# Deeper load buffers for the second part of a hybrid SSD and GLA layer, paid for with DMA scratch

## The chip, the cores and the metric

The kernel runs on one core of a Trainium2 chip. The metric is the device time of one execution in microseconds (us). Lower is better. Engines are named as in the profile: PE is TensorE (matmuls; PEld its weight loads), DVE is VectorE, ACT is ScalarE, POOL is GpSimd, SP is SyncE, which here only issues DMAs.

## The reference: what is computed

One layer of a hybrid decoder with 2048 tokens (and 16 meta tokens ahead of them) and a width of 1024. A normalised input is projected into all branch inputs; two branches (an SSD scan and a gated linear attention scan) give `y_ssd` and `y_gla`; then the branches are projected, gated, added and projected again:

```python
u = rmsnorm(hres, norm_w)
proj = jnp.einsum('bld,dn->bln', u, w_in)          # merge_g is the last 2048 of its columns
...                                                # the two scans give y_ssd and y_gla
branches = jnp.stack([y_ssd, y_gla], axis=2)
branch_proj = jnp.einsum('blnc,ncd->blnd', branches, w_branch)
gates = jax.nn.sigmoid(merge_g.reshape(b, l, N_BRANCH, D_MODEL))
merged = jnp.sum(gates * branch_proj, axis=2)
h = hres + jnp.einsum('bld,de->ble', merged, w_out)
return rmsnorm(h, final_norm_w)[:, N_META:]
```

## The kernel before, in words

The kernel has two parts. The first computes the branch inputs and the scans and leaves `u` and the two `y` in DRAM. The second part, which alone is changed, does the gate projection, the two branch projections and the output projection as large matrix products.

**The second part.** It has seven stages in this order: for each half of the tokens a gate stage, the first branch stage and the second branch stage, then one output stage. Each stage multiplies a right operand of 1024 x 1024 (all its quarters and their sums and differences stay in SBUF for the whole stage) with a left operand that passes by in pairs of row blocks. It does so by a seven product scheme (a 2 x 2 Strassen scheme in Winograd's form): the order of products for each two pairs is `PS = (1, 2, 6, 7, 5, 3, 4)`, each for the one pair and then the other, so that a stage of eight pairs has 56 products and one of four pairs has 28; 280 products in all. A product is 12 matmuls of 128x128 by 128x512: four contraction tiles by three, since every operand is held as a high and a low float32r half.

**What feeds a product.** A right operand tile is loaded raw by SP (`load_b`, line 966, tile `br`), and split by ACT (high half, line 971) and DVE (low half, line 972) into a tile `b`; 28 of them make a stage. The left operand comes by `load_a` (line 978, tile `ar`), POOL makes sums and differences of its quarters (lines 986 to 989, tiles `as`), and ACT and DVE split each into a tile `a` (lines 995 and 996) five products ahead. Products 1, 6, 5 and 3 of a pair gather in the same PSUM bank (`psa`): after product 1, 6 and 5 ACT copies what stands there to SBUF (line 1012, tile `sn`, called the snapshot below), and the next product of that pair may only go on in the bank when the copy is done. Between product 5 of a pair and its product 3 lies one product of the other pair. What comes out is used by the stage's epilogue, for which SP loads gates, partial sums or rows of the input into tiles `io` (lines 1043, 1045 and 1068).

**Who sets the order.** PE's and SP's instructions run in the order of the code. A list of positions sets it: `load_b` for the 28 tiles of the next stage stands at positions from 12 products ahead of the stage on, 0.8 products apart (`pos`), less a lead; `prep_b`, the split, stands at `pos`. The order on ACT, DVE and POOL is made when the program is built, by a scheduler that estimates times. SP's queue is in order: a load that waits for its buffer holds all the loads behind it. Each tile name has a ring of buffers (`bufs`), so a load waits until the tile that many loads back has been read for the last time. Besides, all DMAs of SP and ACT share eight semaphores in turn, and a DMA waits until the one that used its semaphore before has landed.

**Scratch.** A part of SBUF of 16 KB per partition is set aside for descriptors of DMAs that POOL issues. There are two of these in the whole program: the last two stores of `y` (line 878).

Of the kernel before, what the change touches and what calls it, by code (L numbers as in the profile page):

```python
# [7 lines left out]
F32 = mybir.dt.float32  # L8
# [6 lines left out]
P = 128  # L15
# [3 lines left out]
BLK = 512  # L19
# [21 lines left out]
def trunk_kernel(ctx: ExitStack, tc: tile.TileContext, xm, xmt, w_feat, w_tok, w_zm, w_br, w_o,  # L41
                 cf32, cmsk, pvec, fnw, hvec, gw2, out):
    nc = tc.nc
# [5 lines left out]
    def mk(pool, shape, dt, tag, **kw):  # L49
        cnt[0] += 1  # L50
        return pool.tile(shape, dt, tag=tag, name=f"{tag}_{cnt[0]}", **kw)
# [20 lines left out]
    def make_sums(pool, tag, nb, braw, sums, j, c, store):  # L72
        cs = slice(c * HB, (c + 1) * HB)
        pair = [mk(pool, [P, 512], F32, tag, bufs=nb).rearrange("p (i c) -> p i c", i=2) for _ in range(2)]
        for r, (k, t) in zip((t[:, i] for t in pair for i in range(2)), ((0, 1), (0, 0), (1, 1), (1, 0))):
            nc.sync.dma_start(r, braw(4 * k + j, t)[:, cs])
        yield
        (b12, b11), (b22, b21) = [(t[:, 0], t[:, 1]) for t in pair]
        for o, x, y in ((b11, b12, b11), (b12, b22, b12), (b22, b22, b11), (b21, b21, b22)):
            nc.gpsimd.tensor_tensor(o, x, y, op=ALU.subtract)  # L80
        if store is None:
            for dst, src in zip(sums, pair):
                late_store(dst[j][:, :, cs], src, 2)
            return
        yield
        yield
        for dst, src in zip(sums, pair):
            store.dma_start(dst[j][:, :, cs], src)
# [3 lines left out]
    def late_store(dst, src, lag=1):  # L92
        stores.setdefault(step_no[0] + lag, []).append((dst, src))

    def new_sums(name):
        return [[wdram.tile([P, 2, BLK], F32, tag=f"{name}_t{i}_{j}", name=f"{name}_t{i}_{j}", bufs=1)
                 for j in range(4)] for i in range(2)]

    def braw_u(s):
        return lambda k, t: u_left[2 * s + t][k]  # L100

    def braw_y(n, s):
        return lambda k, t: y_left[n][2 * s + t][k]

    def braw_o(k, t):
        return w_o[t, :, k * BLK:(k + 1) * BLK]

    sums = {**{("g", s): (braw_u(s), new_sums(f"gate{s}")) for s in range(nsb)},
            **{("b", n, s): (braw_y(n, s), new_sums(f"br{n}{s}")) for n in range(2) for s in range(nsb)},
            ("o",): (braw_o, new_sums("out"))}  # L110

    beside = {(1, 0): ("o",), (1, 4): ("g", 0)}
    late = []
# [812 lines left out]
    def pool2(name, bufs, **kw):  # L926
        return second.enter_context(tc.tile_pool(name=name, bufs=bufs, reuse_waits="tile", **kw))

    rpl = pool2("raws", 1)
    apl = pool2("aops", 7)  # L930
    bpl = pool2("bops", 4)
    opl = pool2("outs", 1)
# [18 lines left out]
    class Stage:  # L951
# [9 lines left out]
        def load_b(self, p, j):  # L961
            src = {1: lambda j: self.braw(j, 0), 2: lambda j: self.braw(4 + j, 0), 3: lambda j: self.braw(4 + j, 1),
                   4: lambda j: self.sums[1][j][:, 1], 5: lambda j: self.sums[0][j][:, 1],
                   6: lambda j: self.sums[1][j][:, 0], 7: lambda j: self.sums[0][j][:, 0]}[p]
            raw = self.braws[p, j] = mk(rpl, [P, BLK], F32, "br", bufs=5)
            nc.sync.dma_start(raw, src(j))

        def prep_b(self, p, j):
# [5 lines left out]

        def load_a(self, n):
            def raw(i, j):
                t = mk(rpl, [P, 4, P], F32, "ar", bufs=8)
                nc.sync.dma_start(t, self.araw(n, i, j))
                return t

            if n not in self.a:
                self.a[n] = raw(0, 0), raw(0, 1), raw(1, 0)
                return
            (a11, a12, a21), a22 = self.a[n], raw(1, 1)
            s1, s2, s4 = [mk(rpl, [P, 4, P], F32, "as", bufs=6) for _ in range(3)]
            nc.gpsimd.tensor_tensor(s1, a21, a22, op=ALU.add)  # L986
            nc.gpsimd.tensor_tensor(s2, s1, a11, op=ALU.subtract)
            nc.gpsimd.tensor_tensor(a21, a11, a21, op=ALU.subtract)
            nc.gpsimd.tensor_tensor(s4, a12, s2, op=ALU.subtract)
            self.a[n] = {1: a11, 2: a12, 3: s4, 4: a22, 5: s1, 6: s2, 7: a21}  # L990
# [24 lines left out]
                self.use(n, *USES[p], self.ps[n, "b"] if p == 5 else ps, self.snap.get((n, {2: 1, 5: 5, 4: 6}.get(p))))  # L1015

    def io():
        return mk(opl, [P, BLK], F32, "io", bufs=8)

    def total(ps, snap):  # L1020
        if snap is None:
            return ps
        nc.vector.tensor_tensor(snap, snap, ps, op=ALU.add)
        return snap

    def gate_stage(s):
        def use(n, i, t, ps, snap):
            x = total(ps, snap)
            th = io() if snap is None else snap
            nc.scalar.activation(th, x, AF.Tanh, scale=0.5)  # L1030
            store(g_left[2 * s + t][2 * n + i], th)

        return Stage(f"gate{s}", ("g", s), 8,
                     lambda n, i, j: w_feat[T_GATE + 2 * n + i, :, j * BLK:(j + 1) * BLK].rearrange(
                         "p (k c) -> p k c", c=P), use)
# [26 lines left out]
    def out_stage():  # L1062
        fns, res, ssq, done = [], {}, {}, set()

        def fetch(n, i, t):
            r0 = (2 * n + i) * P
            res[n, i, t] = r = io()
            nc.sync.dma_start(r, xm[META + r0:META + r0 + P, t * BLK:(t + 1) * BLK])

        def use(n, i, t, ps, snap):  # L1070
            r0 = (2 * n + i) * P
            r = res[n, i, t]
            done.add((n, i, t))
            x = total(ps, snap)
            nc.vector.scalar_tensor_tensor(r, x, 0.5, r, op0=ALU.mult, op1=ALU.add)
            if (n, i) not in ssq:
                ssq[n, i] = mk(spl, [P, 2], F32, "ssf")
            jk = mk(spl, [P, BLK], BF16, "junk", bufs=1)
            nc.scalar.activation(jk, r, AF.Square, accum_out=ssq[n, i][:, t:t + 1])
            if (n, i, 1 - t) in done:  # L1080
                while len(fns) < 2:
                    fns.append(mk(rpl, [P, BLK], F32, "br", bufs=5))
                    nc.sync.dma_start(fns[-1], fnw[:, (len(fns) - 1) * BLK:len(fns) * BLK].to_broadcast([P, BLK]))
                q = ssq[n, i]
                nc.vector.tensor_tensor(q[:, 0:1], q[:, 0:1], q[:, 1:2], op=ALU.add)
                nc.vector.tensor_scalar(q[:, 0:1], q[:, 0:1], 1.0 / D, EPS, op0=ALU.mult, op1=ALU.add)
                nc.gpsimd.tensor_tensor(q[:, 0:1], q[:, 0:1], mhalf[:, 0:1], op=ALU.pow)
                for hf in range(2):
                    o = res[n, i, hf]
                    nc.vector.scalar_tensor_tensor(o, o, q[:, 0:1], fns[hf], op0=ALU.mult, op1=ALU.mult)  # L1090
                    store(out[r0:r0 + P, hf * BLK:(hf + 1) * BLK], o)

        return Stage("out", ("o",), seq // (2 * P),
                     lambda n, i, j: m_left[(2 * n + i) // 4][j][:, :, (2 * n + i) % 4 * P:((2 * n + i) % 4 + 1) * P],
                     use, fetch, 3)

    stages = []
# [16 lines left out]
    def at(pos, fn):  # L1114
        pos = max(pos, -1)
        todo.setdefault(int(pos // 1), []).append((pos, len(todo), fn))
# [5 lines left out]
    for si, st in enumerate(stages):  # L1122
        for q in range(28):
            p, j = PS[q // 4], q % 4
            pos = begins[si] - 12 + 0.8 * q if si else -0.99 + 0.2 * (q // 4) if q < 16 else 2 * (q // 4 - 4)
            at(pos - (3.2 if si else 0.1), lambda st=st, p=p, j=j: st.load_b(p, j))
            at(pos, lambda st=st, p=p, j=j: st.prep_b(p, j))
    for i, (st, n, p) in enumerate(order):
        if p in USES and st.fetch:
# [2 lines left out]
        at(i - AHEAD if i >= AHEAD else -0.95 + 0.1 * i, lambda st=st, n=n, p=p: st.prep_a(n, p))  # L1132
    begun_at = [begins[3 * s] for s in range(nsb)]
    spots = [g + 9 + 5 * k for g in begun_at for k in range(8)]
    late_sums = [make_sums(opl, "io", 8, *sums[key], j, c, None) for key in late for j in range(4) for c in range(2)]
    for pos, gen in zip(spots, late_sums):
        for k in range(2):
            at(pos + 2 * k, lambda gen=gen: next(gen, None))
# [99 lines left out]
```

## Time and profile before

| | us |
|---|---|
| median of 3 runs | 2309.24 (2306.60 to 2315.05) |
| the profiled execution, its own time | 2308.46 |
| its span in the trace | 2306.7 |
| PE busy | 2232.1 (97% of the span) |
| DVE busy | 1609.6 (70%) |
| ACT busy | 1121.4 (49%) |
| POOL busy | 683.6 (30%) |
| first matmul of the second part | at 1504.6 |
| start of its last matmul | at 2296.4 |

A busy PE says little about how closely its matmuls follow each other: what counts is the time from the start of one matmul to the start of the next, and where it waits. In the tables of windows the columns are the length, then the busy time and the number of instructions of each engine, then the granted clock of PE (1.00 is the full clock), the busy share of the 16 DMA engines and what they moved. In the timelines a number in brackets is the idle time of the engine ahead of the instruction, and what ended it.

### The profile page before, as it was taken

How to read it: one execution, taken by the hardware profiler on the slowest of the kernel's cores; microseconds unless marked ns; L12 is line 12 of the kernel's file. 1: busy time of each engine (PE TensorE's matmuls, PEld its weight loads, DVE VectorE, ACT ScalarE, POOL GpSimd, SP SyncE). 2: the span in 40 equal slices, each digit the busy share in tenths (PEclk: the TensorE clock that was granted, in tenths of full speed). 3: DMA queues.
4: the chain of work that ended last, by engine and by line, in shares of the span. 5: the costliest groups of instructions: out<-in, count | busy, mean ns of one | idle time of the engine just before them, and what ended most of it. 6: DMA issues, size and time to landing. Idle time of an engine off the chain costs nothing.

```text
span 2306.7 us, 36436 instructions
## 1 busy us (share of the span) xinstructions
PE 2232.1 (97%) x12631; PEld 1949.0 (84%) x12631; DVE 1609.6 (70%) x3136; ACT 1121.4 (49%) x2508; POOL 683.6 (30%) x675
## 2 busy tenths in 40 slices
PE   6899999999999999999999999989999999999998
PEld 6899988888888989888988898778787788787886
DVE  5786766687775677676578656664779855778966
ACT  5565554454444445444455334454644545554443
POOL 3344433122221222222122100145424264423341
PEclk9999999999999999999999999999999999999999
DMA  7766865667786676786667644465767866778653
GB/s 260 234 220 219 289 229 205 203 204 230 257 284 193 204 223 213 253 286 215 205 216 230 215 163 156 151 224 200 252 238 261 280 215 217 255 255 273 226 186 110
DMA packets 300809, 515.89 MB, mean 224 GB/s; under 512 B 27616, under 2 KB 143584, under 8 KB 300624
## 3 DMA queue, kind: packets, MB, share of 16 engines
q1 hardware_dynamic: 221840, 422.15, 56.5%
q10 hardware_dynamic: 78624, 90.89, 11.2%
q8 instruction: 99, 1.62, 0.3%
q14 instruction: 86, 0.70, 0.1%
q0 software_dynamic: 160, 0.52, 0.1%
HBM read 366.26 MB, written 147.19 MB: 223 GB/s over the span
## 4 chain that ended last, share of the span: by engine, by line
PE 64%; DVE 12%; DMA 12%; issue 6%; ACT 4%; POOL 1%; SPq 1%; ACTq 0%; DVEq 0%; POOLq 0%
PE pj L189 11%; PE pj L191 11%; PE pj L190 11%; PE psa L189 4%; PE psa L190 4%; PE psa L191 4%; DMA acc<-in_xmt 2%; PE psb L190 2%; PE psb L189 2%; PE psb L191 2%; DMA br<-br_t 2%; PE pc L594 2%; PE pc L758 1%; DVE b L972 1%; PE psc L190 1%
## 5 line engine op out<-in xcount | busy, mean ns | idle before, releaser
L189 PE MATMUL pj<-u,whl 128*128 128x512 f32 (+1 forms) x1184 | 446.0, 377 | 9.5 <-ACT acc L504 4.5
L191 PE MATMUL pj<-u,whl 128*128 128x512 f32 (+1 forms) x1184 | 430.7, 364 | 0.8 <-POOL whl L177 0.8
L190 PE MATMUL pj<-u,whl 128*128 128x512 f32 (+1 forms) x1184 | 430.1, 363 | 0.0
L189 PE MATMUL pj<-whl,u 128*128 128x256 f32 (+1 forms) x992 | 288.7, 291 | 2.4 <-ACT u L252 2.2
L191 PE MATMUL pj<-whl,u 128*128 128x256 f32 (+1 forms) x992 | 282.2, 285 | 0.2 <-DVE u L257 0.2
L190 PE MATMUL pj<-whl,u 128*128 128x256 f32 (+1 forms) x992 | 282.0, 284 | 0.0
L189 PE MATMUL psa<-b,a 128*128 128x512 f32 x640 | 254.0, 397 | 16.4 <-ACT sn L1012 16.2
L189 PEld LDWEIGHTS pj<-u,whl 128*128 128x128 f32 x1184 | 224.5, 190 | 48.4 <-ACT acc L504 5.4
L190 PE MATMUL psa<-b,a 128*128 128x512 f32 x640 | 253.1, 395 | 2.0 <-DVE b L972 2.0
L191 PEld LDWEIGHTS pj<-u,whl 128*128 128x128 f32 x1184 | 224.0, 189 | 36.6 <-POOL whl L177 1.0
L190 PEld LDWEIGHTS pj<-u,whl 128*128 128x128 f32 x1184 | 224.8, 190 | 33.3
L191 PE MATMUL psa<-b,a 128*128 128x512 f32 x640 | 252.6, 395 | 0.0
L996 DVE TENSOR_TENSOR a<-ar,a 128x512 fp32r<-128x512 f32 x160 | 148.1, 930 | 84.3 <-ACT a L995 84.1
L80 POOL TENSOR_TENSOR wr<-wr 128x256 f32<-128x256 f32 x80 | 69.4, 868 | 442.7 <-DMA wr<-u 184.4
L177 POOL TENSOR_TENSOR whl<-wr,whl 128x512 fp32r<-128x512 f32 (+1 forms) x100 | 136.5, 1373 | 195.4 <-ACT whl L176 155.5
L189 PEld LDWEIGHTS pj<-whl,u 128*128 128x128 f32 x992 | 189.6, 191 | 4.1 <-ACT u L252 2.3
L191 PEld LDWEIGHTS pj<-whl,u 128*128 128x128 f32 x992 | 189.6, 191 | 0.8 <-DVE u L257 0.8
L190 PEld LDWEIGHTS pj<-whl,u 128*128 128x128 f32 x992 | 189.8, 191 | 0.4
L972 DVE TENSOR_TENSOR b<-br,b 128x512 fp32r<-128x512 f32 x196 | 148.4, 780 | 43.2 <-ACT b L971 43.1
L986 POOL TENSOR_TENSOR as<-ar,ar 128x512 f32<-128x512 f32 x40 | 59.4, 1484 | 396.2 <-DMA ar<-in_w_br 154.2
L508 DVE SCALAR_TENSOR_TENSOR acc<-cin,hcw,acc 128x512 f32<-128x512 f32 (+1 forms) x192 | 159.6, 831 | 13.9 <-ACT acc L504 11.6
L971 ACT ACTIVATE b<-br 128x512 fp32r<-128x512 f32 x196 | 119.3, 626 | 93.4 <-DMA br<-br_t 41.4
(281 smaller groups left out, 5017.7 us busy)
## 6 DMA issues: line engine op xcount, KB each, us to landing
whl<-k_s SPq DMA_DIRECT2D x96, 512.0 KB, 4.3
whl<-k_g SPq DMA_DIRECT2D x96, 512.0 KB, 4.2
whl<-k_v SPq DMA_DIRECT2D x48, 512.0 KB, 4.0
whl<-k_z SPq DMA_DIRECT2D x36, 512.0 KB, 4.1
wr<-in_w_feat SPq DMA_DIRECT2D x64, 256.0 KB, 4.3
k_s<-whl SPq DMA_DIRECT2D x32, 512.0 KB, 3.7
cb<-cumd ACTq DMA_DIRECT2D x64, 256.0 KB, 5.7
k_g<-whl SPq DMA_DIRECT2D x32, 512.0 KB, 3.9
```

The lines of the kernel that those rows point to most:

```text
L80: nc.gpsimd.tensor_tensor(o, x, y, op=ALU.subtract)
L177: nc.gpsimd.tensor_tensor(hl[:, 1], raw, hl[:, 0].bitcast(F32), op=ALU.subtract)
L189: nc.tensor.matmul(ps, sh, mh, start=first, stop=False, **kw)
L190: nc.tensor.matmul(ps, sh, ml, start=False, stop=False, **kw)
L191: nc.tensor.matmul(ps, sl, mh, start=False, stop=last, **kw)
L508: nc.vector.scalar_tensor_tensor(acc, cin[:, k:k + tt], hcw[:, ti, k:k + 1], acc, op0=ALU.mult, op1=ALU.add)
L594: nc.tensor.matmul(py[:, h * 64:(h + 1) * 64], dm[:, h], xdt[:, h], start=True, stop=True)
L758: nc.tensor.matmul(ps[:, r * P:(r + 1) * P], kq[:, 2 * r * P:(2 * r + 1) * P], kq[:, (2 * r + 1) * P:(2 * r + 2) * P], start=True, stop=True)
L971: nc.scalar.activation(t[:, 0], raw, AF.Copy)
L972: nc.vector.tensor_tensor(t[:, 1], raw, t[:, 0].bitcast(F32), op=ALU.subtract)
L986: nc.gpsimd.tensor_tensor(s1, a21, a22, op=ALU.add)
L996: nc.vector.tensor_tensor(t[:, 1], src, t[:, 0].bitcast(F32), op=ALU.subtract)
```

## The change

The scratch for POOL's DMAs goes from 16 KB to 2 KB per partition. The 14 KB are given to three rings of 2 KB tiles in the second part: raw right operand tiles `br` from 5 to 8, raw left operand tiles `ar` from 8 to 10, epilogue tiles `io` from 8 to 10. `load_b` gets a lead of 5 products instead of 3.2.

```diff
-            raw = self.braws[p, j] = mk(rpl, [P, BLK], F32, "br", bufs=5)
+            raw = self.braws[p, j] = mk(rpl, [P, BLK], F32, "br", bufs=8)
...
-                t = mk(rpl, [P, 4, P], F32, "ar", bufs=8)
+                t = mk(rpl, [P, 4, P], F32, "ar", bufs=10)
...
     def io():
-        return mk(opl, [P, BLK], F32, "io", bufs=8)
+        return mk(opl, [P, BLK], F32, "io", bufs=10)
...
-                    fns.append(mk(rpl, [P, BLK], F32, "br", bufs=5))
+                    fns.append(mk(rpl, [P, BLK], F32, "br", bufs=8))
...
             pos = begins[si] - 12 + 0.8 * q if si else -0.99 + 0.2 * (q // 4) if q < 16 else 2 * (q // 4 - 4)
-            at(pos - (3.2 if si else 0.1), lambda st=st, p=p, j=j: st.load_b(p, j))
+            at(pos - (5 if si else 0.1), lambda st=st, p=p, j=j: st.load_b(p, j))
             at(pos, lambda st=st, p=p, j=j: st.prep_b(p, j))
...
-    late_sums = [make_sums(opl, "io", 8, *sums[key], j, c, None) for key in late for j in range(4) for c in range(2)]
+    late_sums = [make_sums(opl, "io", 10, *sums[key], j, c, None) for key in late for j in range(4) for c in range(2)]
...
-    nc = _bacc.Bacc("TRN2", target_bir_lowering=False, num_devices=1)
+    nc = _bacc.Bacc("TRN2", target_bir_lowering=False, num_devices=1, dynamic_dma_scratch_size=2048)
```

The instructions of every engine are the same in number and kind, and PE's order is the same. SP's order changes where right operands of a next stage are loaded, and the scheduler's order on ACT and DVE changes there with it; up to the second part no engine's order changes.

At the end of the first gate stage, SP's queue held this before (the numbers in names only tell tiles apart: `br_t` is a right operand in DRAM, `in_w_br` the weights that pass as left operands):

```order
L966 DMA br_18693<-br_t_0_176 128x512
L978 DMA ar_18695<-in_w_br 128x512
L978 DMA ar_18697<-in_w_br 128x512
L978 DMA ar_18699<-in_w_br 128x512
L978 DMA ar_18718<-in_w_br 128x512
L966 DMA br_18730<-br_t_1_177 128x512
L966 DMA br_18753<-br_t_2_178 128x512
L966 DMA br_18761<-br_t_3_179 128x512
```

and this now, at the same place:

```order
L966 DMA br_18640<-br_t_0_176 128x512
L966 DMA br_18661<-br_t_1_177 128x512
L978 DMA ar_18682<-in_w_br 128x512
L966 DMA br_18694<-br_t_2_178 128x512
L978 DMA ar_18699<-in_w_br 128x512
L978 DMA ar_18701<-in_w_br 128x512
L978 DMA ar_18703<-in_w_br 128x512
L978 DMA ar_18722<-in_w_br 128x512
L966 DMA br_18731<-br_t_3_179 128x512
```

The loads of the second and third tile (`br_t_1_177`, `br_t_2_178`) stood behind four loads of left operands and now stand ahead of all of these or all but one; the fourth stands where it stood.

On ACT, at the end of the last branch stage, ahead of the output stage, this stood before (`sn_23042` is the snapshot after product 5 of the one pair of the stage's last two, `sn_23086` that of the other pair; `b` are splits of right operands of the output stage, `a` those of left operands):

```order
L971 ACTIVATE b_4117_23140<-br_23028 128x512
L995 ACTIVATE a_23105<-ar_22994 128x512
L971 ACTIVATE b_4122_23167<-br_23066 128x512
L1012 ACTIVATE sn_23042<-psa_22821 128x512
L995 ACTIVATE a_23137<-ar_23068 128x512
L1012 ACTIVATE sn_23086<-psa_22846 128x512
```

and this now:

```order
L971 ACTIVATE b_4120_23146<-br_22973 128x512
L949 DMA m_1_17336<-io_22868 128x512
L995 ACTIVATE a_23064<-ar_22716 128x512
L971 ACTIVATE b_4125_23173<-br_23004 128x512
L971 ACTIVATE b_4128_23197<-br_23029 128x512
L971 ACTIVATE b_4132_23223<-br_23067 128x512
L995 ACTIVATE a_23111<-ar_22998 128x512
L1012 ACTIVATE sn_23046<-psa_22825 128x512
L995 ACTIVATE a_23141<-ar_23072 128x512
L971 ACTIVATE b_4136_23244<-br_23105 128x512
L1012 ACTIVATE sn_23090<-psa_22850 128x512
```

The first snapshot (now `sn_23046`) stands behind two more splits of right operands than before, and the second (`sn_23090`) behind three more.

## The prediction

> **What bounds the kernel now.** I first read the table of windows for the second part without its first and last microseconds, then the waits there, then the timelines at the longest waits.
>
> ```profile
> 1512.00:2297.00 785.00, 768.60 (x3349) 633.19 (x3348) 561.89 (x764) 387.27 (x708) 299.03 (x230) 0.99 0.69 230
> ...
> PE psa L189 <- ACT sn L1012: 16.2, 6, 4.8
> ...
> ACT b L971 <- DMA br<-br_t: 41.4, 28, 4.9
> ```
>
> The waits are total, number and longest one. PE waits here for one thing only, the snapshot (`sn`), six times. Its pace between waits comes from the timeline:
>
> ```profile
> 1647.63 0.39 PE L191 MATMUL psa<-b,a 128*128 128x512 f32 x1
> ...
> 1652.39 0.39 PE L191 MATMUL psa<-b,a 128*128 128x512 f32 x1
> 1655.42 0.80 PE L189 MATMUL psa<-b,a 128*128 128x512 f32 x1 [2.65 <-ACT sn L1012]
> 1656.02 0.63 PE L190 MATMUL psa<-b,a 128*128 128x512 f32 x1
> ...
> 1658.58 0.41 PE L190 MATMUL psa<-b,a 128*128 128x512 f32 x1
> ```
>
> From 1647.63 to 1652.39 there are 21 steps: 0.2267 us each. So 3349 matmuls need 759.2 us, and the window loses 785.0 - 759.2 - 0.4 after the last matmul = about 25 us. The six waits are 16.2 of these; the other 9 are what follows a wait. After the wait of 2.65 us the next matmuls stand 0.43 us apart, and seven steps take 3.16 us, not 1.59. That stall costs 3.03 - 0.23 = 2.80 from start to start, and 1.57 of slow restart: 4.4 us. The other five:
>
> ```profile
> 1540.77 0.50 PE L189 MATMUL psa<-b,a 128*128 128x512 f32 x1 [1.32 <-ACT sn L1012]
> 1737.75 0.50 PE L189 MATMUL psa<-b,a 128*128 128x512 f32 x1 [1.66 <-ACT sn L1012]
> 1814.49 0.50 PE L189 MATMUL psa<-b,a 128*128 128x512 f32 x1 [2.96 <-ACT sn L1012]
> 1971.56 0.50 PE L189 MATMUL psa<-b,a 128*128 128x512 f32 x1 [2.83 <-ACT sn L1012]
> 2125.39 0.39 PE L191 MATMUL psa<-b,a 128*128 128x512 f32 x1
> 2130.55 0.80 PE L189 MATMUL psa<-b,a 128*128 128x512 f32 x1 [4.77 <-ACT sn L1012]
> ...
> 2136.58 0.40 PE L191 MATMUL psa<-b,a 128*128 128x512 f32 x1
> 2125.70:2137.00 11.30, 6.53 (x17) 5.11 (x17) 8.35 (x10) 4.40 (x9) 9.35 (x6) 0.70 0.89 275
> ```
>
> At 2130.55 it is 5.16 - 0.23 = 4.9, and 14 steps that take 6.03 instead of 3.18 us: 7.8 in all, with a granted clock of 0.70. The two waits near 1.5 us cost 1.6 and 1.9 with their first step; what is left of the 25 makes 4.7 each for 1814 and 1971. By place: 1.6 + 4.4 + 1.9 + 4.7 + 4.7 + 7.8 = 25.1 us. All six stand at a stage's end, where the next stage's right operands come in.
>
> Why is the snapshot late? ACT and SP ahead of 1655.42:
>
> ```profile
> 1653.57 1.32 ACT L971 ACTIVATE b<-br 128x512 fp32r<-128x512 f32 x2 [4.22 <-DMA br<-br_t]
> 1654.79 0.58 ACT L1012 ACTIVATE sn<-psa 128x512 f32<-128x512 f32 x1
> ...
> 1656.53 1.38 ACT L971 ACTIVATE b<-br 128x512 fp32r<-128x512 f32 x2 [0.64 <-DMA br<-br_t]
> ...
> 1643.42 6.77 SPq L978 DMA_DIRECT2D ar<-in_w_br  x4
> 1650.25 2.32 SPq L966 DMA_DIRECT2D br<-br_t  x5
> ```
>
> The product that the snapshot copies is long done. The snapshot stands behind two splits in ACT's order, these wait 4.22 us for their load, and SP issued that load only at 1650.25 because four `ar` loads, in the queue ahead of it, took 6.77 us to find buffers. So: loads of `br` late, ACT late, PE late.
>
> **The change, part by part.** Everything up to 1504 is as it was: 0.
>
> Scratch: two stores of `y` use it.
>
> ```profile
> L878 POOL DMA_DIRECT2D y<-gg x2: 548/654/759, 1504.9 to 1507.1; - x2
> L76 SPq DMA_DIRECT2D io<-y x64: 319/378/732, 1534.6 to 1943.5; - x64
> ...
> DMA to landing us min/median/max: 2.0/4.0/9.1
> ```
>
> I take 0. Even if the second store had to wait until the first has landed, a median of 4.0 us for `y`, both would be down long before the first load of `y` at 1534.6: that distance of 27 us is the cover, and without it the cost would be those 4 us, at most 9.1. The 14 KB freed pay for 3 + 2 + 2 tiles of 2 KB, so nothing else shrinks. The pair of end-of-kernel loads into `br` only gets more room: 0.
>
> Start of the first gate stage (1504.6 to 1512): its loads keep their lead of 0.1 product; three more can be out early, but its splits follow part one on ACT. I take 0, with a gain of at most the 2.02 us of this wait:
>
> ```profile
> 1507.40 0.79 PE L190 MATMUL psa<-b,a 128*128 128x512 f32 x1 [2.02 <-DVE b L972]
> ```
>
> `br` from 5 to 8 and the lead: a load may go out when the tile eight loads back, not five, has been split by DVE, and it stands ahead of most of the `ar` loads.
>
> ```profile
> 1638.45 1.29 DVE L972 TENSOR_TENSOR b<-br,b 128x512 fp32r<-128x512 f32 x2
> ...
> SPq L966 <- DVE b L972: 110.6, 88, 13.1
> SPq L978 <- DVE a L996: 102.0, 33, 12.3
> ...
> DMA to landing us min/median/max: 2.4/4.2/7.4
> ```
>
> For `br_t_1_177`, the load issued at 1650.25, the tile eight back was split by 1638.45 + 1.29 = 1639.7. It may go out some 10 us earlier, and land (the last row is for `br`) at 1644 to 1647, ahead of the snapshot's need at 1652.6. The next tile, behind which the snapshot stands now, comes one transfer later. The places at 1737, 1814 and 1971 wait 1.66 to 2.96 us, and their snapshots now stand behind one to three more splits, which at 1655 followed 2.4 us later (1656.53 and 0.6, against 1654.79). They need their loads some 4 to 6 us sooner, and 10 are to be had where the ring frees them as here. At 1540 ACT waits for an `ar`, which two more buffers let out earlier:
>
> ```profile
> 1538.56 0.63 ACT L995 ACTIVATE a<-ar 128x512 fp32r<-128x512 f32 x1 [3.44 <-DMA ar<-in_w_feat]
> ```
>
> I keep 0.25 us at 1540, 1655, 1737 and 1971 for what lands late, and 1 at 1814, where three more splits need the most.
>
> At 2130 the room is smallest: two and three more splits stand ahead of the snapshots.
>
> ```profile
> 2107.74 1.90 DVE L972 TENSOR_TENSOR b<-br,b 128x512 fp32r<-128x512 f32 x3 [1.30 <-ACT b L971]
> ...
> 2129.86 0.90 SPq L966 DMA_DIRECT2D br<-out_t  x2
> ...
> 2104.00:2112.00 8.00, 8.00 (x37) 6.62 (x36) 5.46 (x9) 4.65 (x9) 0.00 (x0) 1.00 1.01 353
> 2112.00:2120.00 8.00, 8.00 (x37) 6.62 (x36) 8.00 (x15) 6.17 (x12) 0.00 (x0) 1.00 0.73 232
> 2120.00:2131.00 11.00, 6.23 (x27) 4.91 (x26) 5.39 (x10) 3.98 (x9) 3.43 (x3) 0.94 1.12 350
> 2104.00:2165.00 61.00, 56.23 (x237) 45.97 (x236) 51.46 (x76) 33.51 (x63) 12.86 (x8) 0.94 0.91 296
> ```
>
> From the first free slots (2108.4, in the group of three splits) 15 loads and 4 stores must pass until the last tile wanted is in. One is 0.262 MB, 0.75 us at 353 GB/s: 14.2 us, so 2122.6, and two more ACT instructions make 2124. PE asks at 2125.6. A margin of 1.6 us is under the spread of landings, so I keep 2 us of wait and 1 of restart; the ends are 0 and 7.8.
>
> A rule to weigh: the Trainium skill, "TensorE: Matmul & The Clock Gate", Part 1, says that the clock halves after an idle window of about 3.4 us. The rows above show half pace after 2.65 us and none after 1.66, so a leftover wait can cost a restart below that figure. By the page the 1 us of restart would go, and the sum would be 1 us lower.
>
> `ar` and `io` from 8 to 10: no term of their own but the 1540 place. They release SP sooner and cost nothing by themselves: the bytes are the same, earlier. What an earlier load meets is the stage's own traffic, which hides under PE's products.
>
> What is late next where the stall at 2130 goes: DVE, busy 51.46 of the 61 us that shrink to 53.2 without the stall (97%). It fits barely, and this is another reason for keeping 3 there.
>
> Sum: kept 3 + 1 + 4 x 0.25 = 5, gain 25.1 - 5 = 20.1, which on 2308.46 (the profiled execution, 1.8 over its span) gives 2288.4. The median of three runs is 0.8 above that execution: 2289. With all six gone it is 2284, with the ends of 2130 and 1814 kept 2297.
>
> **The rivals.** *A: the DMA engines are the limit where it matters.* The stages into the second branch stage and the output stage stall where traffic is dense:
>
> ```profile
> 1805.00:1815.00 10.00, 7.04 (x31) 5.53 (x30) 3.60 (x6) 3.98 (x8) 3.53 (x3) 1.00 1.03 375
> ```
>
> Ahead of 1814 the 16 engines are busy 1.03 of the time and move 375 GB/s; ahead of 2130, 350. If the earlier loads only crowd there, 1814 and 2130 keep their 4.7 and 7.8: gain about 11 to 12, near 2297. Against it: 232 GB/s from 2112 to 2120, which is room that SP's queue, not the DMA engines, leaves unused. The Trainium skill ("SBUF — State Buffer", Summary: rules for kernel authors) tells one to reckon with about 358 GB/s between HBM and SBUF; the rows agree, up to 375, and it speaks for A.
>
> *B: the snapshot waits behind more splits.* It now needs one to three tiles more. If their loads come no earlier, at 1655 it waits for the split that started at 1656.53: snapshot at 1657.2 instead of 1654.8, 2.4 later; at 2130 for the second load issued from 2129.86 (2130.3 + 4.2 + 0.6 = 2135.1, not 2129.9), 5.2 later. Mean 3.8 at six places: 23 slower, 2332. It decides when the loads gain less than those 2.4 to 5.2 us; the 10 us found at 1639.7 speak against it.
>
> *C: nothing happens.* SP's queue is held by something else, `ar` (102.0 us) or the eight semaphores, and loads come earlier just enough to pay for the later place: 2300 to 2312, middle 2308.
>
> **How the numbers follow.** 0.70 for the forecast (2282 to 2295 by its own bounds), 0.14 for A (2294 to 2300), 0.09 for C, 0.07 for B. Half a percent, 11.5 us, is about what a measurement of this kernel can tell from no change, so faster means below 2297.7. That takes the 0.70 and under half of A, 0.06: 0.76 faster. Same: the rest of A and C, 0.17. Slower: B, 0.07. A range of 2282 to 2301 leaves out B, most of C and little else.
>
> **What would show it.** Right: PE's waits for `sn` fall from 16.2 to some 4 us between 1512 and the end, rows with pace 0.43 vanish at 1655, 1814 and 1971, and SP issues `br_t_1_177` near 1640. A: the waits at 1814 and 2130 stay, with DMA shares over 1 ahead of them. B: waits of over 5 us for `sn` behind splits that wait for `br`. The forecast is wrong if ACT's waits for `br` don't fall from 41.4 us, or if a new waiter (DVE's `a` or `b`) appears on PE.

## The result, and the profile after

The changed kernel takes 2326.68 us (median of 6 runs, 2323.51 to 2331.47), against 2309.38 for the kernel before on the same chip. The ratio is 1.0061, with a 95% interval of 1.0042 to 1.0079: 17 us slower in the medians, where 20 us less were forecast. The profiled execution took 2325.64 us. One execution among those below, the profiled one of e4, ran at a granted clock of 0.75 and took 2760 us; e4's median leaves it out, and the table of losses has no column for it.

The second part without its first and last microseconds, in the table of windows of the changed kernel:

```profile
1512.00:2314.00 802.00, 772.79 (x3353) 632.68 (x3351) 574.67 (x764) 382.80 (x707) 299.48 (x230) 0.99 0.67 225
```

The waits in that window (total, number, longest):

```profile
PE psa L189 <- ACT sn L1012: 22.4, 12, 5.1
...
ACT b L971 <- DMA br<-br_t: 9.4, 6, 3.0
PE psb L189 <- DVE sn L1023: 6.7, 6, 1.9
```

3353 matmuls need 760.1 us at 0.2267; 0.2 us follow the last. So this window loses about 42 us (the table below, by product, finds 40.8), where the kernel before lost 25. ACT's waits for `br_t` did what the prediction hoped for, 9.4 us instead of 41.4; those for the right operands of the gate and output stages did not fall (`gate_t` 15.6 us, 14.1 before; `out_t` 11.4, 11.2 before). PE nevertheless waits longer for snapshots (22.4 instead of 16.2), and a new waiter is there, for DVE. SP's queue shows the earlier loads:

```profile
1634.83 1.67 SPq L978 DMA_DIRECT2D ar<-in_w_br  x3
1636.79 1.66 SPq L966 DMA_DIRECT2D br<-br_t  x2
1639.84 0.33 SPq L978 DMA_DIRECT2D ar<-in_w_br  x1
```

The second of the two loads at 1636.79 is the tile that had gone out at 1650.25; it goes out at 1637.67.

Where PE lost its time, by product (the number in the order of the 280 products; start to start less 0.2267, with the slow restart that follows; from one profiled execution of each kernel, in us; the labels are those of the experiments below):

| product | before | after | e1 (br) | e3 (br, ar) | e2 (br, io) | e13 (after, sums on DVE) |
|---|---|---|---|---|---|---|
| 11 | 1.7 | - | - | - | - | 4.8 |
| 52, 53 | 4.4 | 6.5 | 1.6 | 6.8 | 2.1 | - |
| 80 to 83 | 1.9 | 3.1 | 6.5 | 2.4 | 6.6 | - |
| 108 to 111 | 4.8 | 2.1 | 1.6 | 0.5 | 1.8 | - |
| 116 to 120 | - | 2.8 | 1.6 | 2.9 | 1.6 | - |
| 122, 123 | - | 7.9 | - | 7.3 | - | 2.8 |
| 164, 165 | 4.7 | 2.5 | 4.1 | 1.6 | 3.1 | - |
| 192 to 195 | - | 1.7 | 4.5 | 3.2 | 3.8 | - |
| 220 to 223 | 7.8 | 4.2 | 2.2 | 1.4 | 3.3 | - |
| 228 to 233 | - | 2.1 | 1.2 | 1.6 | 3.3 | - |
| 246, 260 | - | 7.9 | - | - | 8.8 | - |
| sum | 25.3 | 40.8 | 23.3 | 27.7 | 34.4 | 7.6 |

The six old places lost 25.3 and the same rows (11; 52 and 53; 80 to 83; 108 to 111; 164 and 165; 220 to 223) now lose 18.4, so they gained 7, not 20. Places with no stall before cost 22. Three places show what happened.

**Product 53: DVE is late.** DVE, POOL, ACT and PE, in this order:

```profile
1647.16 1.78 DVE L996 TENSOR_TENSOR a<-ar,a 128x512 fp32r<-128x512 f32 x1
1648.86 5.18 DVE L972 TENSOR_TENSOR b<-br,b 128x512 fp32r<-128x512 f32 x3
1653.97 1.77 DVE L996 TENSOR_TENSOR a<-ar,a 128x512 fp32r<-128x512 f32 x1
1655.66 1.74 DVE L972 TENSOR_TENSOR b<-br,b 128x512 fp32r<-128x512 f32 x1
1657.33 0.68 DVE L1023 TENSOR_TENSOR sn<-sn,psb 128x512 f32<-128x512 f32 x1
...
1646.76 1.63 POOL L987 TENSOR_TENSOR as<-as,ar 128x512 f32<-128x512 f32 x1
...
1656.82 1.71 POOL L989 TENSOR_TENSOR as<-ar,as 128x512 f32<-128x512 f32 x1
...
1658.04 0.63 ACT L1030 ACTIVATE sn<-sn 128x512 f32<-128x512 f32 x1 [5.01 <-DVE sn L1023]
...
1659.09 0.58 ACT L1012 ACTIVATE sn<-psa 128x512 f32<-128x512 f32 x1
...
1659.72 0.77 PE L189 MATMUL psa<-b,a 128*128 128x512 f32 x1 [4.68 <-ACT sn L1012]
```

A split on DVE takes 1.74 to 1.78 us here, where three took 1.90 together at 2107.74 in the kernel before. Slow splits are not new at this place: before, three of them took 1.77 to 1.79 us each from 1648.06 on. Now six follow each other. POOL makes its sums without a gap from 1645 to 1658. DVE's six splits of this stretch fill ten microseconds, the sum of line 1023 stands behind them, ACT's next epilogue step (line 1030) waits 5.01 us for it, and the snapshot stands behind that. The one DVE instruction that reads PSUM (line 1023) takes its 0.68 us also beside POOL.

**Product 122: two stores in ACT's queue.** POOL, ACT, PE:

```profile
1853.39 1.17 POOL L80 TENSOR_TENSOR io<-io 128x256 f32<-128x256 f32 x1
1854.53 1.73 POOL L987 TENSOR_TENSOR as<-as,ar 128x512 f32<-128x512 f32 x1
1856.22 1.28 POOL L988 TENSOR_TENSOR ar<-ar,ar 128x512 f32<-128x512 f32 x1
1857.48 0.71 POOL L80 TENSOR_TENSOR io<-io,io 128x256 f32<-128x256 f32 x1
...
1858.22 0.54 ACTq L949 DMA_DIRECT2D br_t<-io  x1
1858.81 1.15 ACT L995 ACTIVATE a<-ar 128x512 fp32r<-128x512 f32 x2 [5.68 <-POOL io L80]
1861.26 0.52 ACTq L949 DMA_DIRECT2D br_t<-io  x1
1861.82 0.60 ACT L1012 ACTIVATE sn<-psa 128x512 f32<-128x512 f32 x1 [1.87 <-POOL io L80]
...
1862.47 0.80 PE L189 MATMUL psa<-b,a 128*128 128x512 f32 x1 [5.06 <-ACT sn L1012]
```

ACT issues the stores of the late sums (line 80), and its queue is in order. In the new order two of them stand ahead of the snapshot. They wait for POOL, which alternates late sums with the sums of line 986 to 989.

**Product 246: one small POOL instruction.** After, POOL, DVE, ACT and PE; then POOL before:

```profile
2206.70 1.28 POOL L986 TENSOR_TENSOR as<-ar,ar 128x512 f32<-128x512 f32 x1 [7.78 <-DMA ar<-m]
2207.94 0.55 POOL L1087 TENSOR_TENSOR ssf<-ssf,mhalf 128x1 f32<-128x1 f32 x1
...
2208.53 3.47 DVE L1090 SCALAR_TENSOR_TENSOR io<-io,ssf,br 128x512 f32<-128x512 f32 x2 [5.29 <-POOL ssf L1087]
...
2210.33 2.04 ACTq L949 DMA_DIRECT2D out_h<-io  x2
...
2217.32 0.58 ACT L1012 ACTIVATE sn<-psa 128x512 f32<-128x512 f32 x1
...
2217.95 0.79 PE L189 MATMUL psa<-b,a 128*128 128x512 f32 x1 [4.40 <-ACT sn L1012]
```

```profile
2191.57 0.55 POOL L1087 TENSOR_TENSOR ssf<-ssf,mhalf 128x1 f32<-128x1 f32 x1 [1.96 <-DVE ssf L1086]
2201.39 1.30 POOL L986 TENSOR_TENSOR as<-ar,ar 128x512 f32<-128x512 f32 x1 [9.27 <-DMA ar<-m]
```

The pair has changed places. A sum that waits 7.78 us for a load now holds the power instruction of a row's norm, for which DVE, ACT's store and with it the snapshot wait.

### The profile page after: what moved, and what is told of

Read it like the earlier page. It is cut to its first block, busy times and chain, and to the rows that moved or that the text cites. A ratio compares the mean times of both kernels' runs of the same rounds, so it can differ in the third digit from the quotient of the medians.

```text
span 2323.8 us, 36457 instructions
## 1 busy us (share of the span) xinstructions
PE 2234.9 (96%) x12631; PEld 1947.9 (84%) x12631; DVE 1621.9 (70%) x3136; ACT 1116.8 (48%) x2508; POOL 683.1 (29%) x675
## 3 DMA queue, kind: packets, MB, share of 16 engines
q10 hardware_dynamic: 78624, 90.89, 11.2%
## 4 chain that ended last, share of the span: by engine, by line
PE 59%; DVE 14%; DMA 12%; issue 7%; ACT 4%; POOL 2%; SPq 2%; ACTq 0%; POOLq 0%; DVEq 0%
PE pj L189 11%; PE pj L191 10%; PE pj L190 10%; PE psa L189 4%; PE psa L190 3%; PE psa L191 3%; DMA acc<-in_xmt 2%; PE psb L191 2%; PE psb L190 2%; PE psb L189 2%; PE pc L758 2%; PE pc L594 1%; DVE a L996 1%; DMA m<-io 1%; DVE acc L508 1%
## 5 line engine op out<-in xcount | busy, mean ns | idle before, releaser
L189 PE MATMUL psa<-b,a 128*128 128x512 f32 x640 | 254.6, 398 | 22.7 <-ACT sn L1012 22.4
L972 DVE TENSOR_TENSOR b<-br,b 128x512 fp32r<-128x512 f32 x196 | 160.8, 852 | 17.0 <-ACT b L971 15.9
L189 PEld LDWEIGHTS psa<-b,a 128*128 128x128 f32 x640 | 122.3, 191 | 53.9 <-ACT sn L1012 27.9
```

The source lines that it names most:

```text
L189: nc.tensor.matmul(ps, sh, mh, start=first, stop=False, **kw)
L972: nc.vector.tensor_tensor(t[:, 1], raw, t[:, 0].bitcast(F32), op=ALU.subtract)
```

## The experiments

Theory O: the scheduler, given deeper rings, put other work ahead of snapshots, and that order costs. Theory D: DVE, slowed beside POOL, is what is late. Theory S: earlier `br` loads hold back others in SP's queue. Each result is a median and its ratio to the kernel before, with a 95% interval. The kernel before ran beside every batch (e1 to e4, e5 to e8, e9 to e12, e13 to e16, e17), and its median moved between 2309.4 and 2313.9 us, so a difference of a few us between batches is no finding. Edits are shown shortened.

**The parts of the change.** All four with 2 KB of scratch.

```text
 e1_br:    br 5 -> 8, lead 3.2 -> 5
 e2_brio:  e1 and io 8 -> 10
 e3_brar:  e1 and ar 8 -> 10
 e4_ario:  ar 8 -> 10, io 8 -> 10
```

> Only the right operand part of the change: br 8, lead 5, scratch 2 KB; ar and io stay at 8. Theory O (order: the deeper rings let the scheduler put other work ahead of ACT's snapshots; in the changed kernel two stores of late sums stand ahead of the snapshot of product 122, which cost 8.1 us there): these two stores are behind it again, the stage ends are ordered as in the changed kernel, so 25 us of stalls become about 19 and little is new: 2299 to 2312, middle 2304. Theory D (DVE: earlier splits run while POOL makes sums, where a DVE instruction took 1.78 us and not 0.69): stage ends as in the changed kernel, 2304 to 2315. Theory S (SP: earlier br loads hold back ar and io loads behind them): with fewer ar and io buffers it is worse than the changed kernel, 2327 or more.

> The change without the ar ring (ar stays at 8). Its ACT order is that of the changed kernel but for four instructions, among them the two stores ahead of the snapshot of product 122, which are behind it here. Theory O: 8 us less than the changed kernel, 2318 (2313 to 2321). Theory D: the DVE order is the same but for four, so the same time, 2324 to 2329. Theory S: ar loads wait for buffers again as in the kernel before, 2327 to 2335.

> The change without the io ring (io stays at 8). One of the two stores is ahead of the snapshot of product 122, and fewer splits ahead of those of products 116, 117, 228 and 229. Theory O: some 4 us of 122 stay and 2 to 3 us at the others go: 2317 (2312 to 2322). Theory D: 2324 to 2329, the stage ends are the same. Theory S: 2320 to 2330.

> Only ar 10 and io 10, scratch 2 KB; br 5 and lead 3.2 as before. ACT's order at the stage ends is that of the kernel before. Theory O: the snapshots keep their old place and the old waits, slightly less since SP is held less by ar: 2300 to 2310, middle 2306. Theory D: no earlier splits, so no more of them beside POOL: 2309 or slightly less. Theory S (SP's queue is what makes the loads late): up to half of the 25 us go, 2297 to 2303.

e1: 2310.38, ratio to before 0.9998 (0.9985 to 1.0010). e2: 2322.58, 1.0052 (1.0032 to 1.0072). e3: 2314.69, 1.0018 (1.0004 to 1.0032). e4: 2325.66, 1.0062 (1.0038 to 1.0086). So `br` and its lead bring nothing, `io` adds 12 us to that, `ar` 4, and these two alone cost as much as the whole change. Theory S falls: with `br` alone it should have been worst.

e2 was expected by theory O to lose the stall at 122, and did. Its time lies 5 us above what O made of that, between O and D: its profile loses 3.5 us more than the changed kernel's at 80 to 83, and 2.1 more at 192 to 195. e3 lies where theory O had it, though the one store left ahead of the snapshot costs 7.3 us at 122 and not 4. The table shows the two new stalls apart: 122 comes with `ar` 10, 246 with `io` 10.

e4 contradicts all three expectations. Its profile gives no losses to compare, but it shows the order: POOL's two pairs (see product 246) stand swapped as in the changed kernel, while both stores stand behind the snapshot of product 122. So the trace bears out one of the two new stalls and not the other, and what makes up the rest of e4's 14 us stays open.

In e1 the waits were:

```profile
ACT b L971 <- DMA br<-br_t: 24.3, 12, 6.1
...
PE psa L189 <- ACT sn L1012: 16.2, 9, 2.7
```

ACT's waits for `br_t` fell from 41.4 to 24.3, but PE's for the snapshot stayed at 16.2, now nine of them.

**The two new stalls, undone one by one.**

```diff
 e5_two_stores (after; line 949, at step 125 only)
-                nc.scalar.dma_start(dst, src)
+                with issue_after(last_snapshot): nc.scalar.dma_start(dst, src)
 e6_pool_pair (after; line 986)
-            nc.gpsimd.tensor_tensor(s1, a21, a22, op=ALU.add)
+            with issue_after(last_power): nc.gpsimd.tensor_tensor(s1, a21, a22, op=ALU.add)
```

> The changed kernel with one edit: the two stores of late sums that ACT issues around product 122 stand behind the snapshots of products 120 and 121 again; no other instruction moves on any engine. Theory O (order): the 7.9 us of product 122 go and nothing else changes, 2319 (2316 to 2321). Rival (POOL is late whatever the order, and PE waits for the next thing): 2324 or more.

> The changed kernel with POOL's two swapped pairs put back: the small power instruction of a row's norm (line 1087) stands ahead of the sum that waits for a load of ar, at products 246 and 260; two stores on ACT move by one place with it. Theory O: the 7.0 and 0.9 us there go, 2319 (2316 to 2321). Rival (the wait at 246 comes from late ar loads alone, and the swap is beside it): 2324 or more.

e5: 2317.31, 1.0017 (0.9999 to 1.0036), and in its profile 122 and 123 lose 0.5 us instead of 7.9. e6: 2318.13, 1.0018 (1.0001 to 1.0034); 246 loses 2.0 instead of 7.0. Two moved instructions on ACT are worth 9 us, and two swapped pairs on POOL 9, both as theory O expected; with the pairs, two ACT stores moved by one place and four of DVE's instructions of line 1090 by two. Together this would be all of the 17, but no run has both edits, and each of the two gains is uncertain by some 6 us (an estimate from the intervals). In e6 product 53 also lost only 1.7 us, with its order unchanged, so part of e6's gain may not come from the pairs.

**Snapshots first.** A rule for the scheduler (`issue_after` keeps an instruction behind another in its engine's order, and nothing more): on ACT no split of a right operand ahead of a snapshot that the code has earlier.

```diff
 e7_snap (before), e8_br_snap (e1); line 971
-            nc.scalar.activation(t[:, 0], raw, AF.Copy)
+            with issue_after(last_snapshot): nc.scalar.activation(t[:, 0], raw, AF.Copy)
```

> The kernel before (16 KB scratch, br 5, ar 8, io 8, lead 3.2) with one rule for the scheduler: on ACT a split of a right operand is not put ahead of a snapshot that comes before it in the code. At the stage ends four to nine splits that stood ahead of the critical snapshots stand behind them. Theory O: five of the six stalls go (the one at product 11 stays, it waits for an ar load), so of 25 us some 5 stay: 2291 (2285 to 2299). Rival Q (loads are late, and PE will wait for the operands themselves a few products on): 2304 to 2314. If DVE, which splits the low halves, gets too late by it: over 2314.

> The right operand part alone (br 8, lead 5, scratch 2 KB) with the same rule for ACT. Theory O: the ring's new place for the snapshots no longer matters, and loads are early: 2289 (2283 to 2297), equal to the rule without the ring or up to 4 us less. Rival Q: the ring is what helps here, 2295, and the rule without it 2304 to 2314.

e7: 2325.91, 1.0056 (1.0034 to 1.0078): theory O missed by 35 us. ACT now waits in another place, for left operands:

```profile
ACT a L995 <- DMA ar<-in_w_br: 40.0, 13, 4.5
```

The time lies where the expectation put a DVE that gets too late, but PE waits only 0.2 us for DVE there. I read it as SP's queue held longer, since later splits free the five `br` buffers later: SP's waits for DVE's splits of `br` (line 972) went from 110.6 us to 237.4. No run isolates this.

e8: 2306.61, 0.9966 (0.9949 to 0.9983). With eight buffers the rule helps by 4 us (7 by the ratios), not the 20 expected. Two thirds of PE's waits that are left are for DVE:

```profile
PE psa L191 <- DVE a L996: 5.2, 2, 3.2
PE psa L189 <- ACT sn L1012: 4.5, 4, 2.3
PE psb L190 <- DVE b L972: 3.7, 2, 1.8
```

**Scratch, sums on DVE, all rules, more br.**

```text
 e9_scratch:    before with dynamic_dma_scratch_size=2048 alone
 e10_sums_dve:  e8 and lines 986 to 989: nc.gpsimd -> nc.vector
 e11_all_rules: after, with the rules of e6 and e8 and that of e5 for all stores
 e12_br12:      e8 with br 12, lead 6, splits 0.7 products apart
```

> Only the scratch, 16 KB to 2 KB; rings, lead and every engine's order are those of the kernel before. All theories: no change, within 3 us of the kernel before. Rival (the scratch itself costs, by its size or by where it moves the buffers in SBUF): 3 to 6 us slower, as the first parts of the changed kernels' profiles were 1 to 5 us longer.

> The right operand part with the rule for ACT (2306.6), and POOL's four sums of a left operand's quarters (lines 986 to 989) made by DVE. Theory D (while POOL makes sums a DVE instruction takes 1.78 us and not 0.69, and DVE is what is late at the stage ends): DVE gets 160 x 0.69 = 110 us more to do but loses some 95 us of slow instructions, in the places where it is late; most of the 13 us in which PE waits for DVE's a and b go: 2297 (2290 to 2303). Rival (DVE's total is what counts): 2312 to 2325.

> The whole change (br 8, ar 10, io 10, lead 5, scratch 2 KB) with three rules: on ACT neither a split of a right operand nor a store goes ahead of a snapshot that comes before it in the code, and on POOL no sum goes ahead of a norm's power instruction. Theory O (the ar and io rings cost only by the order that they led to): as the right operand part with its rule, 2306 (2300 to 2311). Rival (the deeper rings cost by themselves, by traffic): 2316 to 2324.

> The right operand part with the rule for ACT, all 14 KB given to br (12 buffers), lead 6, splits 0.7 products apart instead of 0.8. If the last splits are what is late at products 96 and 208 (2.1 us each, PE waits for DVE's b): 2302 (2297 to 2306). If DVE has no room for a denser row of splits: the waits at 113 and 225 (5.0 and 3.9) grow, 2307 to 2314.

e9: 2311.77, 1.0001 (0.9987 to 1.0015): the scratch costs nothing. e10: 2300.31, 0.9953 (0.9936 to 0.9970), for theory D. e11: 2300.29, 0.9955 (0.9941 to 0.9969): the deeper rings cost only by the orders that came with them. e12: 2303.66, 0.9962 (0.9949 to 0.9976), as expected if the last splits are what is late, but e8's interval overlaps with its own; in its profile the DVE waits are gone, but products 109 and 221 lose 7.0 and 7.7, the first behind a split of an `ar` that came late.

**Order or DVE?** The last question was why `br`, whose loads do come earlier, gained nothing.

```text
 e13_after_dve:  after, lines 986 to 989: nc.gpsimd -> nc.vector, no rule
 e14_br_rules:   e1 with the three rules of e11
 e15_all_dve:    after, rules for splits and stores, sums on DVE
 e16_before_dve: before, sums on DVE
 e17_dve_later:  e13, but sums made ahead of product 12 stay on POOL
```

> The changed kernel as it is (no rule on any order), but with the sums of lines 986 to 989 on DVE. It tells how much of the stage ends' loss there is the slow DVE beside POOL. Theory D: the stalls at 53, 82, 83, 111, 193 to 195 and 221 to 223 (some 16 us, most of them end with a DVE instruction) go for the most part, and 246 too, as POOL has no sum to put ahead of the power instruction; 122 stays, its stores wait for POOL's late sums: 2308 (2303 to 2314). Theory O alone (splits ahead of snapshots are what costs, at any speed of DVE): only 246 goes, 2318 to 2322.

> The right operand part (ar and io stay at 8) with all three rules. It tells whether ar 10 and io 10 bring anything once the orders are held. If they do: some 5 us slower than the whole change with the rules (2300.3), 2305 (2302 to 2309). If the rules on stores and sums brought it, and the rings nothing: 2300 (2297 to 2302).

> The whole change with the rules for splits and stores on ACT, and the sums on DVE: the two edits that gained most, together. Their remaining stalls lie at different places but for the start and one at products 235 and 236: 2295 (2291 to 2299). If both had gained the same us: 2300.

> The kernel before with the sums on DVE, nothing else. Its six stalls wait for loads of br and ar behind a held queue, not for DVE. Theory of late loads: they stay, 2306 to 2312. If DVE beside POOL is what frees the br and ar buffers late, and so holds the queue: loads come earlier and half of the stalls go, 2296 to 2302.

> The changed kernel with the sums on DVE, but for those that are made ahead of product 12, which stay on POOL. In the run with all sums on DVE the second part began some 4 us later than the first part's end alone accounts for, since ACT's first splits of left operands stand ahead of the first part's last work and wait for DVE's sums, and PE lost 4.8 us at product 11. If both come from these first sums: 2290 (2287 to 2294). If the stall at product 11 only moves on, or the late begin is chance: 2295 to 2299.

e13: 2298.04, 0.9926 (0.9906 to 0.9947), 29 us below the changed kernel and under what even theory D gave. Of the 33 us that e13 loses less than the changed kernel, 25 lie at the stage ends and in the ten products behind them; 13 lie at 122 and 246, where POOL's own queue was what was late, and product 11 gives 5 back. e16: 2320.57, 1.0036 (1.0022 to 1.0050): the same edit makes the kernel before slower. So without POOL's sums beside DVE the change is worth 22.5 us (2320.6 to 2298.0). DVE's splits in the kernel before, in the changed one and in e13 (busy, mean ns, idle before), all from 1525 to 2280:

```profile
L996 DVE TENSOR_TENSOR a<-ar,a 128x512 fp32r<-128x512 f32 x154 | 144.1, 940 | 84.0 <-ACT a L995 83.8
L972 DVE TENSOR_TENSOR b<-br,b 128x512 fp32r<-128x512 f32 x177 | 136.1, 790 | 40.9 <-ACT b L971 40.9
```

```profile
L972 DVE TENSOR_TENSOR b<-br,b 128x512 fp32r<-128x512 f32 x177 | 148.7, 870 | 14.7 <-ACT b L971 13.7 <-DMA io<-g 1.0
L996 DVE TENSOR_TENSOR a<-ar,a 128x512 fp32r<-128x512 f32 x152 | 144.3, 958 | 71.8 <-ACT a L995 70.8
```

```profile
L972 DVE TENSOR_TENSOR b<-br,b 128x512 fp32r<-128x512 f32 x184 | 122.8, 695 | 13.1 <-ACT b L971 12.9
L996 DVE TENSOR_TENSOR a<-ar,a 128x512 fp32r<-128x512 f32 x155 | 109.4, 711 | 52.0 <-ACT a L995 51.3
```

At the place of product 53, in e13, the epilogue step that waited 5.01 us for DVE waits 0.16:

```profile
1666.26 0.63 ACT L1030 ACTIVATE sn<-sn 128x512 f32<-128x512 f32 x1 [0.16 <-DVE sn L1023]
```

And PE's and ACT's waits in the second part, e13 and then e16:

```profile
ACT b L971 <- DMA br<-br_t: 10.0, 8, 2.3
...
PE psa L189 <- ACT sn L1012: 5.3, 3, 3.1
```

```profile
ACT b L971 <- DMA br<-br_t: 40.7, 30, 3.5
...
PE psa L189 <- ACT sn L1012: 21.9, 9, 5.1
```

In e16 the loads are as late as before, and a fast DVE doesn't help: the stage ends lose 22.5 us by the count of the table, 23.6 before. What makes it slower lies at product 11 and at 122 to 124, which lose 11 us where the kernel before lost 1.7. In e13 the splits that the scheduler put ahead of the snapshots are still there, and cost nothing, because neither a load nor DVE holds them: so at the stage ends it is not the order alone, as theory O said, but the order times a DVE at 0.4 of its pace.

e14: 2302.12, 0.9957 (0.9940 to 0.9973), no different from e11: `ar` and `io` at 10 are harmless once the order is held, and bring nothing that shows. e15: 2300.03, 0.9940 (0.9920 to 0.9961): the rules add nothing to e13. e17: 2288.44 (2286.55 to 2291.46), 0.9894 (0.9877 to 0.9910), the best of all, as expected for the case that both late items came from the first sums. Its second part begins at 1506.1, where e13's begins at 1515.2, and product 11 loses nothing. The second part in the table of windows, and then PE's only wait there:

```profile
1512.00:2275.00 763.00, 761.31 (x3353) 629.44 (x3351) 570.90 (x909) 386.38 (x707) 77.55 (x86) 1.00 0.70 237
```

```profile
PE psa L189 <- ACT sn L1012: 1.2, 1, 1.2
```

DVE has 145 instructions more than in the changed kernel's window and is busy for 570.90 us instead of 574.67.

## Why the prediction was wrong

- *What bounds the kernel:* right at five places: waits for snapshots, behind splits, behind late loads, behind a held queue. e16 shows it once more, and e13 what is gained when all links are loosened. The sixth, at 1540, is product 11, well inside the first gate stage of 56 products, and not at a stage's end as the prediction says of all six; ACT waits for an `ar` there.
- *Scratch, 0:* right (e9).
- *`br` and lead, loads some 10 us earlier:* right for the tile that was followed, which goes out 12.6 us earlier (1650.25 to 1637.67), but this was a favourable one. Counted against PE's products of 2.72 us, the 28 tiles of a stage go out 6 to 11 us earlier on average in the changed kernel, single ones between 0 and 28, and 4 to 7 in e1; at 1734.97 and 2054.11 in e1 ACT still waits 5.4 and 6.1 us for a `br_t`.
- *The stalls gone but for 5 us:* wrong. The old places still lose 18.4. e1 gained 2 us of loss in its profile and nothing in its time.
- *The step that failed first, "what is late next":* DVE was named, and sized as 51.46 us of work in 53.2, with 3 us kept, and at the other stage ends it had no term. That took the busy time for a fixed amount of work. It depends on what POOL does at that moment: a split that takes 0.69 us alone takes up to 1.78 beside POOL's sums, so that the snapshots of the changed kernel stand behind a late DVE. With POOL's sums on DVE (e13) the stage ends lose nothing. The sign was in the kernel before, in the tile view of `br` that the prediction reads for its loads, as a maximum beside a median (minimum, median, maximum in ns):

```profile
L972 DVE TENSOR_TENSOR b<-br,b x196: 675/685/1784, 1506.7 to 2163.5; 128x512 fp32r<-128x512 f32 x196
```

The Trainium skill has the rule that spoke against this change, and I did not weigh it: "SBUF — State Buffer", Summary: rules for kernel authors, says that when a DVE instruction has two inputs in SBUF and GpSimd reads SBUF, the later one is blocked until the other is done. The trace agrees: 1.78 instead of 0.69 us for a split with two SBUF inputs, beside POOL sums of 1.3 to 1.7 us, and 0.68 for the one with an input in PSUM.

- *The second failed step, "`ar` and `io`: no term of their own":* 12 us for `io` (e2 less e1) and 4 for `ar` (e3 less e1); about 16 for both (the result less e1). I followed the new order at the stage ends only, and on ACT and DVE only; POOL's order changed too. The swapped pair on POOL and the two stores on ACT stand where the kernel had no stall, and so where I did not look.
- *Rival A (DMA engines the limit):* wrong. Its two places lost 2.1 (108 to 111) and 4.2 us (220 to 223), not the 4.7 and 7.8 that it kept, and in e13, with the same transfers, nothing. *Rival B (snapshots behind more splits):* its sign was right and its mechanism partly: in e1 products 80, 81, 165 and 192 wait that way. Its price, 23 us at six places, was not what was paid. *Rival C* fits e1 alone, not the whole change.
- *Product 11 to be cured by `ar`:* not shown; in e1, with `ar` at 8, it has no stall either. Why product 53 costs 6.8 in e3 and 1.6 in e1 stays open; DVE is slow in both.

## What to carry to other kernels

A deeper ring under a scheduler that estimates times is not only a relaxed wait: it reorders every in-order engine, so the whole new order has to be read, above all for stores and small instructions that come to stand behind a wait. Look at a duration's maximum beside its median before its sum is used as a need for time. And work on an idle engine is not free if it slows the busy one: here moving most of the sums from POOL to the busier DVE left DVE's busy time as it was, and the earlier loads paid in full (2288 us), where holding the order alone gave 2300.

## What the runs showed of the hardware that was not expected

A two-input SBUF instruction on DVE takes up to 2.6 times as long (1.78 against 0.69 us) while POOL makes sums of the same size; beside the same sums, line 1023 with an input in PSUM does not (0.68). From 1525 to 2280 us the mean of line 996's splits of `ar` fell from 958 to 711 ns when POOL's sums were taken away.

The first part's length differs between executions with the same order on every engine: the second part's first matmul came at 1504.6 in the profile before and at 1510.1 in e9, whose times are the same, and at 1505.2 and 1510.8 in e5 and e6, which have the same scratch. Single profiles of this kernel are therefore compared by the losses of their second part, and times by medians.
